# The weights' sums of the last product are queued behind taps and spread over the up projection; the held products and the outputs at the end get a fixed order

## The chip, the cores and the metric

The kernel runs on one NeuronCore of a Trainium2 chip. The metric is the device time of one execution in microseconds, as the median of several runs. The engines are TensorE (PE in the profile, with its weight loads as PEld), VectorE (DVE), ScalarE (ACT) and GpSimd (POOL); SyncE (SP) only issues DMAs here. Each engine takes its instructions in the order of its own queue, and a DMA is issued by an instruction that stands in the queue of SP, ACT or POOL.

## The reference, cut to what matters

The kernel computes one layer of a streaming encoder for 512 tokens of width 1024: four parallel mixers with gates, a cross-attention into 256 memory tokens, and a gated MLP. Only the MLP is touched by the change:

```
hf = rms_norm(x, norm_ffn_pre)                            # 512 x 1024
u = dwconv_causal(hf @ w_up, ffn_dw) + ffn_dw_b           # w_up 1024 x 5632, taps of width 3 per channel
u_g, u_v = split(u, 2, axis=-1)                           # 2816 each
yff = (silu(u_g) * u_v) @ w_down                          # w_down 2816 x 1024
x = x + rms_norm(yff, norm_ffn_post)
```

All of it is float32.

## The kernel before

Every product is made of three matmuls in a rounded format (`mm3`): each operand is split into a high part (a cast, on ACT) and a low part (a subtraction, mostly on DVE), and high x high, high x low and low x high are added up in PSUM. Weights are loaded as float32 by SP into raw tiles `wr` (2 buffers), and cast (L183) and subtracted (L184) into `wh` and `wl` (4 buffers each), three jobs ahead of the product that uses them (`run_blocks`).

The kernel is written in program order, but a planner, which simulates the engines, lays out the order of each engine's instructions: what is ready early in its simulation may be put ahead of what is written before it. On the chip the queues then keep that order, and semaphores make them wait.

**Up projection** (`up_jobs`). The 5632 channels come as 44 chunks of 128, n = 0 to 43, taken alternately from the gate half (i = 0) and the value half (i = 1). One chunk is one group of 24 matmuls of 128 x 512 (8 blocks of the width 1024, three matmuls each). The products go to four PSUM banks, two of tag `mm` and two of tag `av`, in turn, so that a group needs the bank of the group four before it. In `done`, ACT writes the bank into `c` with the last tap and the bias (L1290), and DVE adds the two other taps from the bank (`taps`, L519); after that the bank is free. Behind a value chunk come tanh (L1294), two products on DVE (L1295, L1297) into the tiles `qa` or `qb`, and behind every second of these POOL makes sums of activations (`activation_sums`, L1338 to L1341).

**Down projection** (`down_jobs`). The product with `w_down` is made by a scheme with seven products of half size in place of eight (Strassen's, in Winograd's form). The 22 blocks of 128 rows of `w_down` are taken as 11 pairs. For each pair four sums of the weights' quarters are needed. They are made ahead, during the up projection: `weight_pair(q)` has POOL load two blocks into two tiles `wp` (tag `dw`, 4 buffers), `weight_sums(q)` has DVE make four sums in place (L1351 to L1354) and POOL store the tiles to a DRAM tensor `sums` (L1356). In program order `weight_sums(q)` follows `done` of chunk n = 6 + 3q, and `weight_pair(q + 1)` follows that. The tag `dw` is later used by the down projection's own raw tiles, which SP loads (L1373) from `w_down` and from `sums`, and which ACT (L1378) and DVE (L1379) split into `wh` and `wl`, or, for one of the sums, into a tile `n4` in the space of a used-up `qa`.

The down projection has two phases over the 11 pairs. Phase 0 has four products per pair (M1, M6, M5, M7), two tiles of 128 rows each; phase 1 has three (M2, M3, M4). Activations are split into slots in the space of `hth` and `htl`, 4 of them. In phase 1 the products of the last four pairs are held back (`hold`) and made at the end, one result after the other, in `ends`: `whole` makes the 12 held matmuls of one result in one bank and adds the bank to what phase 0 left (L1491); `result` has ACT square it with a sum per row (L1428), POOL make the norm's factor (L262, L265) where both halves of a token tile are there, and DVE multiply by the gain (L1467); `finish` has DVE multiply by the factor and add the residual (L1476), and SP store it (L1477). There are four token tiles of 128; M4 belongs to tiles 2 and 3, M2 and M3 to tiles 0 and 1.

Of the kernel before, what the change touches and what calls it, by code (L numbers as in the profile page):

```python
# [16 lines left out]
F32 = mybir.dt.float32  # L17
F32R = mybir.dt.float32r
AF = mybir.ActivationFunctionType
ALU = mybir.AluOpType  # L20
# [4 lines left out]
P = 128  # L25
S = 512
D = 1024
# [6 lines left out]
NF = DFF // P  # L34
# [48 lines left out]
def hybrid_layer(ctx: ExitStack, tc: tile.TileContext, a: dict, out: bass.AP):  # L83
    nc = tc.nc
    V, A, G, PE, SP = nc.vector, nc.scalar, nc.gpsimd, nc.tensor, nc.sync
# [22 lines left out]
    w_up, w_down = a["w_up"][0], a["w_down"][0]  # L108
# [19 lines left out]
    for i in range(8):  # L128
        n = ("wh", "wl")[i % 2]
# [3 lines left out]
        elif i < 6:  # L133
            n = ("fz_raw", "fz", "fe", "fu", "fd")[i - 1]
# [7 lines left out]
    def weights_tile(kind):  # L142

        i = w_used[kind]
        w_used[kind] += 1
        return w_tiles.pop((kind, i), None) or gp.tile([P, WB], F32R, tag=f"{kind}{i % 4}", name=kind)
# [43 lines left out]
    def cols(w, c0, n=P, k0=0, nk=NK):  # L190

        return w[k0 * P:(k0 + nk) * P, c0:c0 + n].rearrange("(k p) c -> p k c", p=P), [P, nk, n]
# [104 lines left out]
    m1 = tc.tile_pool(name="m1", bufs=1)  # L297
# [181 lines left out]
    def pc(name, j=0, n=1):  # L479
        i, base = where[name]  # L480
        return par[i][:, base + j:base + j + n]
# [33 lines left out]
    def taps(dst, src, w, n):  # L515

        for k in range(n - 1):
            s = n - 1 - k
            V.scalar_tensor_tensor(dst[:, s:], src[:, :S - s], w(k), dst[:, s:], ALU.mult, ALU.add)  # L519


    conv_u, conv_y = y8(F32), y8(F32)
# [744 lines left out]


    sums = dram.tile([NF // 2 * P, 2 * D], F32, name="sums")

    def open_ffn():
        bg.drain("n1")
# [10 lines left out]
    def up_jobs():  # L1283
        st, held = {}, []

        def done(j, i, ps):
            if i == 0:
                st[j] = ns.fp.tile([P, 2, S], F32, tag="c", name="c", bufs=2)
            c, ch = st[j], i * NF + j
            A.activation(c[:, i], ps, AF.Identity, bias=pc("fb", ch), scale=pc("fdw2", ch))  # L1290
            taps(c[:, i], ps, lambda k: pc("fdw01", k * 44 + ch), 3)
            if i == 1:
                th = ns.fp.tile([P, S], F32, tag="th", name="th")
                A.activation(th, c[:, 0], AF.Tanh, scale=0.5)  # L1294
                V.scalar_tensor_tensor(th, th, 1.0, c[:, 0], ALU.add, ALU.mult)  # L1295
                x = ns.quart[j // 2]
                V.scalar_tensor_tensor(x[j % 2][:, 0:2].rearrange("p a b -> p (a b)"), th, 0.5, c[:, 1],  # L1297
                                       ALU.mult, ALU.mult)
                if j % 2:
                    activation_sums(*x)  # L1300


        for n in range(2 * NF):
            def body(hi, lo, n=n):
                j, i = divmod(n, 2)
                if n > 3:
                    ps = bank()
                    channel_major(ps, (hi, lo), ns.hf)
                    done(j, i, ps)
                    if n % 3 == 0 and n // 3 - 2 < NF // 2:  # L1310
                        weight_sums(n // 3 - 2)
                        if n // 3 - 1 < NF // 2:
                            weight_pair(n // 3 - 1)
                    return
                if n == 0:
                    bg.drain("n0")
                ps = bank(("mm", "sc")[n % 2])
                (channel_major if n else by_pass)(ps, (hi, lo), ns.hf, slice(0, S // 2))
                held.append((j, i, ps, (hi, lo)))
                if n == 3:  # L1320
                    open_ffn()
                    for j, i, ps, w in held:
                        (channel_major if i or j else by_pass)(ps, w, ns.hf, slice(S // 2, S))
                        done(j, i, ps)
                    weight_pair(0)
            yield *cols(w_up, n % 2 * DFF + n // 2 * P), body, V, same, HALF_SHIFT if n < 4 else 0


# [12 lines left out]
        G.tensor_tensor(z[:, 2], z[:, 0], x[:, 1], ALU.subtract)  # L1341

    def weight_pair(q):
        ns.pair = [ns.fp.tile([P, D], F32, tag="dw", name="wp", bufs=4) for _ in range(2)]
        for i in range(2):
            G.dma_start(ns.pair[i], w_down[(2 * q + i) * P:(2 * q + i + 1) * P, :])

    def weight_sums(q):

        (b11, b12), (b21, b22) = ((x[:, :S], x[:, S:]) for x in ns.pair)  # L1350
        V.tensor_tensor(b22, b22, b12, ALU.subtract)  # L1351
        V.tensor_tensor(b12, b12, b11, ALU.subtract)
        V.tensor_tensor(b11, b22, b11, ALU.add)
        V.tensor_tensor(b21, b21, b11, ALU.subtract)  # L1354
        for i in range(2):
            G.dma_start(sums[q * P:(q + 1) * P, i * D:(i + 1) * D], ns.pair[i])  # L1356

    def down_jobs():
        pairs, hold, half = NF // 2, 4, S
# [21 lines left out]
        def activations(phase, q):  # L1381

            if (phase, q) == (0, 0):
                hi, lo = (gp.tile([P, WB], F32R, tag="wr", name="wr", bufs=2) for _ in range(2))
            else:
                if "slots" not in parts:
                    parts["slots"] = [t[:, i * 4:i * 4 + 4].rearrange("p a b -> p (a b)") for t in new_ht()
                                      for i in range(2)]
                slot = parts["slots"][(phase * pairs + q - 1) % 4]
                hi, lo = slot[:, :D], slot[:, D:]  # L1390
            n = 4 - phase
            hi, lo = hi[:, :n * 256], lo[:, :n * 256]
            split_to(hi, lo, ns.quart[q][phase].rearrange("p a b -> p (a b)"))
            form = dict(a=n, b=256)
            parts[phase, q] = hi.rearrange("p (a b) -> p a b", **form), lo.rearrange("p (a b) -> p a b", **form)

        def weights(phase, q, job):
            n = 2 * (phase * pairs + q) + job
            load(n + 3)
            if job == 0:  # L1400
                activations(phase, q)
            raw = raws[n]
            if (phase, job) == (1, 1):
                both = ns.fp.tile([P, D], F32R, tag=f"qa{q}", name="n4")
                both = both[:, :half], both[:, half:]
                split_to(*both, raw[:, :half])
                return [both],
            hi, lo = weights_tile("wh")[:, :D], weights_tile("wl")[:, :D]
            split_to(hi, lo, raw)
            return [(hi[:, i * half:(i + 1) * half], lo[:, i * half:(i + 1) * half]) for i in range(2)],  # L1410

# [46 lines left out]
        def result(t, i, x, dst, pieces=1):  # L1458

            ms[t, i] = square(x, i, pieces)  # L1460
            r = None
            if (t, 1 - i) in ms:
                *early, last = ms[t, 1 - i] + ms[t, i]
                if len(early) == 2:
                    G.tensor_tensor(early[0], early[0], early[1], ALU.add)
                r = rstd_of(ns.fp, [early[0], last])
            V.tensor_tensor(dst, x, ns.post[:, gains[i]], ALU.mult)  # L1467
            return r

        def finish(t, halves, r):  # L1470
            for i in halves:
                o = halves[i]
                n = S // 2 if (t, i) == (1, 1) else S
                for c in range(0, S, n):
                    d = slice(i * S + c, i * S + c + n)
                    V.scalar_tensor_tensor(o[:, c:c + n], o[:, c:c + n], r, ns.out[t][:, d], ALU.mult, ALU.add)  # L1476
                    SP.dma_start(out[t * P:(t + 1) * P, d], o[:, c:c + n])  # L1477

        def ends():

            m1, u, z7, z = (parts[n] for n in ("m1", "u", "z7", "z"))

            def whole(name, t, x, pieces=1):

                for c in range(pieces):
                    cut = slice(c * S // pieces, (c + 1) * S // pieces)
                    for q, job, ws in held:
                        for (n, a), w in zip(work[1, job], ws):
                            if n == name:
                                step(name, t, q, a, w, 1, cut)  # L1490
                    V.tensor_tensor(x[:, cut], x[:, cut], banks[name][t][:, cut], ALU.add)  # L1491
                return x

            for t in range(2):
                x = whole("M4", t, z7[:, t])
                finish(2 + t, {1: z[:, t], 0: x}, result(2 + t, 0, x, x))
            for t in range(2):
                x = whole("M2", t, m1[:, t])
                result(t, 0, x, x)
                x = whole("M3", t, u[:, t])  # L1500
                finish(t, {0: m1[:, t], 1: x}, result(t, 1, x, x))

        def body(phase, q, job, ws):
            if (phase, q, job) == (0, 0, 0):
# [66 lines left out]
```

## Time and profile before

| | |
|---|---|
| median of 3 runs | 1074.48 us (1073.96 to 1076.75) |
| profiled execution, its own time | 1080.23 us |
| its span | 1078.4 us |
| granted TensorE clock, mean | 0.995 |
| up projection, first full group to last | 735.8 to 962.3 us |
| 24 matmuls of 128 x 512 in a row | 5.44 us |
| last output issued | 1073.1 us |

The profile is of one execution. Times are in microseconds from the start of the span. A line of a timeline gives start, duration, engine, line of the kernel, operation, what it writes and reads, and in brackets the idle time of the engine ahead of it with what ended that. Instructions on one engine overlap a little, so the distance between two starts is shorter than a duration: 0.227 us between two matmuls whose records last 0.39, and 0.60 us between two DVE additions of 128 x 512 whose records last 0.69. PE's ends are modelled. Some matmul records are missing.

### The profile page before, as it was taken

The page shows a single profiled execution, that of the slowest core. Times are in us where ns is not written, and L with a number is a line of the kernel's source. Part 1 is how long each engine was busy: PE and PEld are TensorE (multiplying, and loading weights), DVE is VectorE, ACT ScalarE, POOL GpSimd, SP SyncE. Part 2 cuts the span into 40 slices and gives each one's busy share as a digit, 9 for nine tenths or more (in the row PEclk, how much of TensorE's full clock was granted, in tenths as well). Part 3 has the DMA queues.
Part 4 walks back from the last instruction along what each step waited for, and adds up shares of the span by engine and source line. Part 5 has one row for each costly group of instructions (what it writes and reads, how often), then busy time and mean ns, then how long its engine had stood idle before and what let it go on. Part 6 is the DMA issues. An engine that isn't in the chain of part 4 may idle for free.

```text
span 1078.4 us, 14440 instructions
## 1 busy us (share of the span) xinstructions
PE 1058.9 (98%) x5387; PEld 899.4 (83%) x5387; DVE 758.1 (70%) x1211; ACT 488.5 (45%) x809; POOL 172.7 (16%) x277
## 2 busy tenths in 40 slices
PE   9999999999999999999999999999998999999995
PEld 8888888888888988888888899998886788888884
DVE  7899996466666467767464486868778686677785
ACT  5322222467464365655443265644322343445671
POOL 4000001000101023323000130132333121111002
PEclk9999999999999999999999999999999999999998
DMA  6433433332222243233255343146889843226662
GB/s 203 117 98 91 90 105 95 94 98 78 59 81 79 63 134 98 79 98 115 62 176 173 120 139 97 59 154 215 268 285 292 269 118 98 79 78 192 215 189 78
DMA packets 158523, 141.04 MB, mean 131 GB/s; under 512 B 5055, under 2 KB 134700, under 8 KB 158453
## 3 DMA queue, kind: packets, MB, share of 16 engines
q1 hardware_dynamic: 149555, 108.50, 34.2%
q0 software_dynamic: 8896, 31.61, 8.8%
q8 instruction: 42, 0.69, 0.3%
q14 instruction: 28, 0.23, 0.1%
q10 hardware_dynamic: 2, 0.00, 0.0%
HBM read 126.45 MB, written 13.65 MB: 130 GB/s over the span
## 4 chain that ended last, share of the span: by engine, by line
PE 85%; DMA 7%; DVE 3%; issue 2%; POOL 1%; ACT 1%; POOLq 0%; DVEq 0%; ACTq 0%
PE ps_mm L225 45%; PE ps_av L225 25%; PE ps_sc L225 7%; DMA sums<-wp 4%; PE ps_tr L229 3%; PE ps_tr L225 2%; DMA wp<-in_w_down 2%; DVE wl L184 1%; PE ps_mm L432 1%; ACT wh L183 0%; DVE c L519 0%; PE ps_av L432 0%; PE ps_mm L374 0%; DMA wr<-in_w_gate 0%; DMA wr<-in_w_in 0%
## 5 line engine op out<-in xcount | busy, mean ns | idle before, releaser
L183 ACT CAST wh<-wr 128x1024 fp32r<-128x1024 f32 (+1 forms) x150 | 156.9, 1048 | 289.0 <-PE ps_mm L225 140.3
L184 DVE TENSOR_TENSOR wl<-wr,wh 128x1024 fp32r<-128x1024 f32 (+1 forms) x150 | 186.0, 1242 | 112.8 <-ACT wh L183 112.4
L225 PE MATMUL ps_mm<-hth,wh 128*128 128x512 f32 (+1 forms) x616 | 231.6, 382 | 4.3 <-DVE c L519 3.8
L225 PE MATMUL ps_mm<-hth,wl 128*128 128x512 f32 (+1 forms) x616 | 230.0, 380 | 0.0
L225 PE MATMUL ps_mm<-htl,wh 128*128 128x512 f32 (+1 forms) x616 | 229.9, 380 | 0.0
L225 PEld LDWEIGHTS ps_mm<-hth,wh 128*128 128x128 f32 x616 | 114.3, 188 | 25.9 <-issue 4.6
L225 PEld LDWEIGHTS ps_mm<-hth,wl 128*128 128x128 f32 x616 | 114.0, 188 | 21.1
L225 PEld LDWEIGHTS ps_mm<-htl,wh 128*128 128x128 f32 x616 | 114.1, 188 | 20.4 <-DVE htl L153 0.2
L225 PE MATMUL ps_av<-hth,wh 128*128 128x512 f32 (+1 forms) x328 | 123.3, 376 | 2.5 <-DVE c L519 2.5
L225 PE MATMUL ps_av<-htl,wh 128*128 128x512 f32 (+1 forms) x328 | 123.0, 375 | 0.0
L225 PE MATMUL ps_av<-hth,wl 128*128 128x512 f32 (+1 forms) x328 | 122.8, 374 | 0.0
L585 DVE SCALAR_TENSOR_TENSOR y<-y,par,y 128x499 f32<-128x499 f32 (+28 forms) x120 | 82.4, 730 | 0.2
L225 PEld LDWEIGHTS ps_av<-hth,wh 128*128 128x128 f32 x328 | 62.0, 189 | 13.9 <-ACT c L1290 2.9
L225 PEld LDWEIGHTS ps_av<-hth,wl 128*128 128x128 f32 x328 | 62.0, 189 | 11.1
L225 PEld LDWEIGHTS ps_av<-htl,wh 128*128 128x128 f32 x328 | 62.1, 189 | 10.8
L225 PE MATMUL ps_mm<-y,wh 128*128 128x512 f32 x192 | 61.2, 394 | 0.0
L1379 DVE TENSOR_TENSOR wl<-dw,wh 128x1024 fp32r<-128x1024 f32 x33 | 41.4, 1260 | 13.4 <-ACT wh L1378 13.3
L1378 ACT CAST wh<-dw 128x1024 fp32r<-128x1024 f32 x33 | 34.5, 1052 | 23.2 <-PE ps_tr L225 8.4
L1294 ACT ACTIVATE th<-c 128x512 f32<-128x512 f32 x22 | 13.9, 632 | 62.4 <-DVE c L519 59.7
L225 PEld LDWEIGHTS ps_mm<-y,wh 128*128 128x128 f32 x192 | 35.4, 188 | 6.8
L908 POOL TENSOR_SCALAR fbias<-ck,cq 128x128 f32<-128x128 f32 (+3 forms) x32 | 27.4, 861 | 68.3 <-DVE st L914 60.5
L225 PE MATMUL ps_mm<-y,wl 128*128 128x512 f32 x96 | 37.6, 392 | 0.0
(426 smaller groups left out, 2026.3 us busy)
## 6 DMA issues: line engine op xcount, KB each, us to landing
wr<-in_w_up SPq DMA_DIRECT2D x44, 512.0 KB
wr<-in_w_in SPq DMA_DIRECT2D x38, 512.0 KB
wr<-in_w_gate SPq DMA_DIRECT2D x32, 512.0 KB
wp<-in_w_down POOLq DMA_DIRECT2D x22, 512.0 KB, 6.2
sums<-wp POOLq DMA_DIRECT2D x22, 512.0 KB, 7.2
dw<-sums SPq DMA_DIRECT2D x44, 256.0 KB
wr<-in_w_branch SPq DMA_DIRECT2D x16, 512.0 KB
dw<-in_w_down SPq DMA_DIRECT2D x11, 512.0 KB
```

The source lines that it names most:

```text
L183: order(A.copy(hi, raw[:, :n]))
L184: low.tensor_tensor(lo, raw[:, :n], hi.bitcast(F32), ALU.subtract)
L225: PE.matmul(ps, lhs, rhs, start=start, stop=stop)
L229: PE.transpose(ps, x, ident[:n, :n])
L432: keep(PE.matmul(banks[c][:, :S // 2], w[p == 1][:, k, c * P:(c + 1) * P], ht[p == 2][:, i * 4 + k, :S // 2], start=(i, p, k) == (0, 0, 0) ...
L585: V.scalar_tensor_tensor(dst[:, s:], src[:, :S - s], pc("conv_dw", k * 4 + j), dst[:, s:], ALU.mult, ALU.add)
L908: G.tensor_scalar(bias[:, :w], ck[j][:, :w], -1.0, cq[:, qt, head:head + 1], ALU.mult, ALU.add)
L1294: A.activation(th, c[:, 0], AF.Tanh, scale=0.5)
L1378: A.copy(hi, x)
L1379: V.tensor_tensor(lo, x, hi.bitcast(F32), ALU.subtract)
```

## The change

`taps` now gives back its last instruction, and `done` keeps it. The DVE instructions of `weight_sums(q)` are bound to stand behind the last tap instruction of chunk n = 6 + 3q on DVE's queue (`tc.issue_after`), so that the planner cannot lay them ahead of it. `weight_pair` is called two pairs ahead in place of one: pairs 0 and 1 both after chunk 3, and pair q + 2 after the sums of pair q.

In the down projection the last pair's activations of phase 1 go to tiles in the space of `qa0` and `qa1`, and its split weights to two tiles of the tag `dw`, where before they took the next slot and the next `wh` and `wl`.

In `ends` the order is written out and kept on PE, DVE, ACT and POOL (`tc.manual_schedule`): M4 of tile 2, M4 of tile 3, then M2 and M3 of tile 0, M2 and M3 of tile 1. The outputs of a token tile (`finish`) stand behind the addition, square and gain of the next product.

```
--- before.py
+++ after.py
@@ -516,7 +516,8 @@
 
         for k in range(n - 1):
             s = n - 1 - k
-            V.scalar_tensor_tensor(dst[:, s:], src[:, :S - s], w(k), dst[:, s:], ALU.mult, ALU.add)
+            ins = V.scalar_tensor_tensor(dst[:, s:], src[:, :S - s], w(k), dst[:, s:], ALU.mult, ALU.add)
+        return ins
 
 
     conv_u, conv_y = y8(F32), y8(F32)
@@ -1267,6 +1268,7 @@
 
 
     sums = dram.tile([NF // 2 * P, 2 * D], F32, name="sums")
+    ns.pair = {}
 
     def open_ffn():
         bg.drain("n1")
@@ -1288,7 +1290,7 @@
                 st[j] = ns.fp.tile([P, 2, S], F32, tag="c", name="c", bufs=2)
             c, ch = st[j], i * NF + j
             A.activation(c[:, i], ps, AF.Identity, bias=pc("fb", ch), scale=pc("fdw2", ch))
-            taps(c[:, i], ps, lambda k: pc("fdw01", k * 44 + ch), 3)
+            st["last"] = taps(c[:, i], ps, lambda k: pc("fdw01", k * 44 + ch), 3).ins
             if i == 1:
                 th = ns.fp.tile([P, S], F32, tag="th", name="th")
                 A.activation(th, c[:, 0], AF.Tanh, scale=0.5)
@@ -1307,10 +1309,12 @@
                     ps = bank()
                     channel_major(ps, (hi, lo), ns.hf)
                     done(j, i, ps)
-                    if n % 3 == 0 and n // 3 - 2 < NF // 2:
-                        weight_sums(n // 3 - 2)
-                        if n // 3 - 1 < NF // 2:
-                            weight_pair(n // 3 - 1)
+                    q = n // 3 - 2
+                    if n % 3 == 0 and q < NF // 2:
+                        with tc.issue_after(st["last"]):
+                            weight_sums(q)
+                        if q + 2 < NF // 2:
+                            weight_pair(q + 2)
                     return
                 if n == 0:
                     bg.drain("n0")
@@ -1323,6 +1327,7 @@
                         (channel_major if i or j else by_pass)(ps, w, ns.hf, slice(S // 2, S))
                         done(j, i, ps)
                     weight_pair(0)
+                    weight_pair(1)
             yield *cols(w_up, n % 2 * DFF + n // 2 * P), body, V, same, HALF_SHIFT if n < 4 else 0
 
 
@@ -1341,19 +1346,20 @@
         G.tensor_tensor(z[:, 2], z[:, 0], x[:, 1], ALU.subtract)
 
     def weight_pair(q):
-        ns.pair = [ns.fp.tile([P, D], F32, tag="dw", name="wp", bufs=4) for _ in range(2)]
+        pair = ns.pair[q] = [ns.fp.tile([P, D], F32, tag="dw", name="wp", bufs=4) for _ in range(2)]
         for i in range(2):
-            G.dma_start(ns.pair[i], w_down[(2 * q + i) * P:(2 * q + i + 1) * P, :])
+            G.dma_start(pair[i], w_down[(2 * q + i) * P:(2 * q + i + 1) * P, :])
 
     def weight_sums(q):
 
-        (b11, b12), (b21, b22) = ((x[:, :S], x[:, S:]) for x in ns.pair)
+        pair = ns.pair.pop(q)
+        (b11, b12), (b21, b22) = ((x[:, :S], x[:, S:]) for x in pair)
         V.tensor_tensor(b22, b22, b12, ALU.subtract)
         V.tensor_tensor(b12, b12, b11, ALU.subtract)
         V.tensor_tensor(b11, b22, b11, ALU.add)
         V.tensor_tensor(b21, b21, b11, ALU.subtract)
         for i in range(2):
-            G.dma_start(sums[q * P:(q + 1) * P, i * D:(i + 1) * D], ns.pair[i])
+            G.dma_start(sums[q * P:(q + 1) * P, i * D:(i + 1) * D], pair[i])
 
     def down_jobs():
         pairs, hold, half = NF // 2, 4, S
@@ -1382,6 +1388,8 @@
 
             if (phase, q) == (0, 0):
                 hi, lo = (gp.tile([P, WB], F32R, tag="wr", name="wr", bufs=2) for _ in range(2))
+            elif (phase, q) == (1, pairs - 1):
+                hi, lo = (ns.fp.tile([P, D], F32R, tag=f"qa{i}", name="a3") for i in range(2))
             else:
                 if "slots" not in parts:
                     parts["slots"] = [t[:, i * 4:i * 4 + 4].rearrange("p a b -> p (a b)") for t in new_ht()
@@ -1405,7 +1413,10 @@
                 both = both[:, :half], both[:, half:]
                 split_to(*both, raw[:, :half])
                 return [both],
-            hi, lo = weights_tile("wh")[:, :D], weights_tile("wl")[:, :D]
+            if (phase, q) == (1, pairs - 1):
+                hi, lo = (ns.fp.tile([P, D], F32R, tag="dw", name="dwr", bufs=4) for _ in range(2))
+            else:
+                hi, lo = weights_tile("wh")[:, :D], weights_tile("wl")[:, :D]
             split_to(hi, lo, raw)
             return [(hi[:, i * half:(i + 1) * half], lo[:, i * half:(i + 1) * half]) for i in range(2)],
 
@@ -1491,14 +1502,19 @@
                     V.tensor_tensor(x[:, cut], x[:, cut], banks[name][t][:, cut], ALU.add)
                 return x
 
-            for t in range(2):
-                x = whole("M4", t, z7[:, t])
-                finish(2 + t, {1: z[:, t], 0: x}, result(2 + t, 0, x, x))
-            for t in range(2):
-                x = whole("M2", t, m1[:, t])
-                result(t, 0, x, x)
-                x = whole("M3", t, u[:, t])
-                finish(t, {0: m1[:, t], 1: x}, result(t, 1, x, x))
+            waiting = None
+            with tc.manual_schedule(engines={e.engine for e in (PE, V, A, G)}):
+                for name, t, i, x in (("M4", 0, 0, z7), ("M4", 1, 0, z7), ("M2", 0, 0, m1), ("M3", 0, 1, u),
+                                      ("M2", 1, 0, m1), ("M3", 1, 1, u)):
+                    token = t + 2 * (name == "M4")
+                    x = whole(name, t, x[:, t])
+                    r = result(token, i, x, x)
+                    if waiting:
+                        finish(*waiting)
+                        waiting = None
+                    if r is not None:
+                        waiting = token, {1: z[:, t], 0: x} if name == "M4" else {0: m1[:, t], 1: x}, r
+                finish(*waiting)
 
         def body(phase, q, job, ws):
             if (phase, q, job) == (0, 0, 0):
```

## The prediction

> **What bounds the kernel now.** I read the page first: its head and the busy time of TensorE (PE).
>
> ```profile
> span 1078.4 us, 14440 instructions
> PE 1058.9 (98%) x5387; PEld 899.4 (83%) x5387; DVE 758.1 (70%) x1211; ACT 488.5 (45%) x809; POOL 172.7 (16%) x277
> ```
>
> PE is busy for 98% of the span: only a place where PE waits, or what lies behind its last matmul, can give time back. So next came the waits, PE's own for the whole run, then all engines' for 725 to 860 us (engine, line, waited for: us in total, times, longest).
>
> ```profile
> PE ps_mm L225 <- DVE c L519: 3.8, 2, 2.3
> PE ps_av L225 <- DVE c L519: 2.5, 1, 2.5
> ...
> ACT wh L183 <- DMA wr<-in_w_up: 38.4, 12, 7.0
> POOL wp L1346 <- DMA sums<-wp: 35.8, 13, 6.6
> DVE wp L1351 <- DMA wp<-in_w_down: 14.1, 5, 4.8
> ```
>
> PE waits three times for taps (L519), which free its banks, and all three lie in the up projection. VectorE (DVE) itself waits for down weights (L1351), GpSimd (POOL) for stores of sums, ScalarE (ACT) for up weights. The timelines of DVE, then PE, around the longest one (start, duration, in brackets idle before and releaser):
>
> ```profile
> 834.06 1.52 DVE L519 SCALAR_TENSOR_TENSOR c<-ps_mm,par,c 128x510 f32<-128x510 f32 x2
> 840.37 0.69 DVE L1351 TENSOR_TENSOR wp<-wp 128x512 f32<-128x512 f32 x1 [4.79 <-DMA wp<-in_w_down]
> ...
> 845.30 0.75 DVE L519 SCALAR_TENSOR_TENSOR c<-ps_av,par,c 128x511 f32<-128x511 f32 x1
> ```
>
> ```profile
> 843.30 0.39 PE L225 MATMUL ps_mm<-hth,wl 128*128 128x512 f32 x1
> 846.19 0.76 PE L225 MATMUL ps_av<-hth,wh 128*128 128x512 f32 x1 [2.51 <-DVE c L519]
> 846.75 0.63 PE L225 MATMUL ps_av<-htl,wh 128*128 128x512 f32 x1
> ```
>
> The sums stand ahead of taps on DVE's queue. DVE sits 4.79 us until the weights land, the taps end at 846.05, and PE starts at 846.19. The windows of 20 us show why the weights land late (PE, PEld, DVE, ACT, POOL busy; clock; DMA share; GB/s):
>
> ```profile
> 820.00:840.00 20.00, 17.68 (x79) 14.32 (x78) 14.20 (x19) 6.32 (x8) 7.07 (x12) 1.00 0.91 286
> 840.00:860.00 20.00, 17.49 (x71) 14.09 (x70) 14.81 (x20) 5.82 (x7) 4.91 (x6) 0.91 0.88 280
> 900.00:920.00 20.00, 20.00 (x90) 16.54 (x89) 11.84 (x15) 7.86 (x10) 2.94 (x4) 1.00 0.36 105
> ```
>
> The planner runs all 11 pairs between 732 and 846, one per 10.4 us, and the DMA engines are 0.9 busy; afterwards they idle. Last, the end:
>
> ```profile
> 1066.82 0.39 PE L225 MATMUL ps_tr<-wh,hth 128*128 128x512 f32 x1
> ...
> 1068.15 0.74 DVE L1476 SCALAR_TENSOR_TENSOR o<-o,st_r,res 128x512 f32<-128x512 f32 x1
> 1068.81 0.68 DVE L1491 TENSOR_TENSOR o<-o,ps_tr 128x512 f32<-128x512 f32 x1
> ```
>
> The last addition starts 1.76 us after PE is done (1067.05, 0.23 after the last matmul's start), because outputs of the token tile before it stand ahead on DVE.
>
> **The change, part by part.**
>
> *Sums behind taps (moved).* Each pair issues 4 DVE subtractions or additions (0.60 us apart, 2.4 us), two stores from POOL (0.54 us each, 7.2 us to landing) and later two loads (0.54 each, 6.2 to landing). Pair q now runs behind the taps of group n = 6+3q, one pair per three groups of 24 matmuls (3 x 5.44 = 16.3 us), the last at n = 36. The work is the same; it moves past taps on DVE and stands ahead only of later ones.
> What it removes: the three PE waits. Start to start, PE loses 1.88-0.23, 2.72-0.23 and 2.89-0.23 us, that is 1.65+2.49+2.66 = 6.80. Behind the first two, one start each is 0.08 late: 0.15. Behind the third, eight starts take 3.50 us in place of 8 x 0.227 = 1.81 (granted clock 0.50 from 847 to 849): 1.69. Sum 8.64 us.
> [...]
>
> *What is late next.* DVE's load per three groups: three splits at 1.14, six taps at 0.66, three products of a chunk (two per two groups, 0.60 each, 1.8), sums 2.4: 11.6 of 16.3 us, so taps keep up. DMA: up weights 0.52 MB per 5.44 us are 96 GB/s, a pair's 2.10 MB per 16.3 us are 129, together 225 against 280 to 307 in the stretch that stalls.
>
> *Loads two pairs ahead (moved).* Pair q+2 takes pair q's buffers: store 7.2 and load 6.2 end 13.4 us after sums q, and sums q+2 come 32.6 us after them. Its wait stands on POOL, ahead of the activation sums (L1338 to 1341), which nobody needs before the down projection. Pairs 0 and 1 are loaded at 721 to 724 as now. Cost nothing, cover 19 us.
>
> *Later first loads of the down projection.* They reuse pairs 9 and 10's buffers, so SP's queue issues them not at 842 but when those are stored: group 4 starts at 735.8, so group 36 ends at 735.8+33 x 5.44 = 915.3, taps 2.3, sums 2.4, store 7.2: 927; landed by 934. The first split of down weights, now at 946.9, comes at about 938. Cost nothing, by 4 us and the weights that are cast three groups ahead.
>
> *Buffers for the last pair, order of the end.* Pair 10's split weights and activations go to tiles that are free, so ACT no longer waits for PE (0.24 us at 1049.57, off the path). In the fixed order, PE's 72 held matmuls take 72 x 0.2267 = 16.32 us, as now; the first product needs pair 10 after nine of them, 2.0 us in. Those activations are ready 2.0 us in now, with that wait ahead of them: no loss. DVE does per product an addition, a wait for ACT's square, a multiplication (1.53+0.61 = 2.14 us); a finish adds 1.32. From the second product's end at 5.44: 3.46+3.46+2.14+3.46 = 12.52, so the last addition starts 17.96 us in, 1.64 after PE's end against 1.76 now. Gain 0.12 us; bounds are 1.76 (DVE free at PE's end) and -1.7 (one finish and one wait for ACT more ahead of it).
>
> Sum: 1080.23 - 8.64 - 0.12 = 1071.5 for the profiled execution. That one lies 5.75 us above the median of the runs shown (1074.48). PE has no other gap over 0.3 us than these waits, the first 1.3 us and the tail, so a part of the 5.75 may be longer waits, as they hang on DMA landings. Bounds: none of it (gain 8.76, 1065.7) or all (3.0, 1071.5). The nearest row is the spread of the runs, 1076.75-1074.48 = 2.27: I take the waits as that much shorter in a median run. 1074.48 - 8.76 + 2.27 = 1068.0.
>
> **The rivals.**
>
> *A part of the waits stays.* For it: ACT waits 38.4 us for up weights, not touched directly. Against: from 860 on, with the DMA engines under half busy, PE does not wait once. Half of 6.4 (8.64 less 2.27) stays: 1068.0+3.2 = 1071.2.
>
> *No effect.* DVE's order changes but DMA, not order, holds the taps; or a new wait takes the sum. Against it: L1351 itself shows the wait. 1074.5.
>
> *Slower: up weights behind down loads on SP.* SP's queue is in order, and the planner may place the loads that wait for pair 10's store ahead of the last up weights; it placed down loads among them at 842 to 854. Then after group 36: taps 2.3, sums 2.4, store 7.2, landing 6.2, cast and split 2.3 = 20.4 us until the next weights, less 5.44 for each group whose weights were issued already. Now the last of 44 up loads is issued at 932.2, when PE is in group 38 of 43, so 4.6 are ahead and nothing shows. With one ahead PE loses 15.0 and the time is 1068.0+15.0 = 1083.0; it decides from two ahead down (9.5 lost, 1077.5).
>
> *More.* DVE is free at PE's end and the waits are as in the profile: 1074.48-8.64-1.76 = 1064.1.
>
> **How the numbers follow.** A measurement can tell about 0.3%, 3.2 us: 1071.3 to 1077.7 is no change. Forecast 0.62 (own range 1065.7 to 1071.5), a part stays 0.12, no effect 0.08, slower by SP's queue 0.10, more 0.08. The range 1063.5 to 1074.5 leaves out the slower case and edges. Faster: 0.62+0.08 and 0.08 of the part case, 0.78; same 0.12; slower 0.10.
>
> **What the profile after would show.** Right: no wait of PE on L519, no wait of L1351 on DMA, the last sums after 915, clock 1.00 throughout, DMA share near 0.7 from 760 to 920, the last addition 1.6 us behind PE. Wrong: PE waiting for weights between groups 37 and 43, for taps elsewhere, or at the start of the held products.

## The result, and the profile after

The changed kernel takes 1071.42 us as the median of 20 runs (1070.42 to 1075.30), the kernel before 1077.59 in 20 runs beside them (1073.96 to 1084.59). The ratio is 0.9942, 95% interval 0.9928 to 0.9957: 6.2 us faster, and the whole interval lies beyond the 0.3% that the prediction counts as no change. The profiled execution took 1070.76 us, its span 1069.0, against 1080.23 and 1078.4 before.

The page of the changed kernel: span, busy time, and the chain that ended last by engine, which gave PE 85% and DMA 7% before.

```profile
span 1069.0 us, 14449 instructions
PE 1056.0 (99%) x5387; PEld 898.2 (84%) x5387; DVE 764.4 (72%) x1211; ACT 489.2 (46%) x809; POOL 171.1 (16%) x277
...
PE 98%; DVE 1%; ACT 0%; issue 0%; POOL 0%; POOLq 0%; DVEq 0%; ACTq 0%
```

The waits of the changed kernel, PE's own for the whole run, then two lines of all engines' for 720 to 960 us (waited for: us in total, times, longest). Lines have moved by a few: the sums are now L1357 to L1360.

```profile
PE ps_mm L374 <- DVE e L325: 1.3, 1, 1.3
PE ps_mm L225 <- ACT hth L152: 0.2, 1, 0.2
...
POOL wp L1351 <- DMA sums<-wp: 28.4, 15, 3.3
ACT wh L183 <- DMA wr<-in_w_up: 1.4, 2, 1.0
```

PE waits for the first operands and 0.2 us once; no wait for taps is left. DVE has no wait for down weights in this stretch, and ACT's for up weights has gone from 38.4 us (725 to 860) to 1.4. DVE's timeline at one pair (start, duration), and the windows of 20 us that answer to those before (PE, PEld, DVE, ACT, POOL busy; clock; DMA share; GB/s):

```profile
835.07 1.53 DVE L519 SCALAR_TENSOR_TENSOR c<-ps_av,par,c 128x510 f32<-128x510 f32 x2
836.51 0.69 DVE L1357 TENSOR_TENSOR wp<-wp 128x512 f32<-128x512 f32 x1
...
840.61 0.68 DVE L1360 TENSOR_TENSOR wp<-wp 128x512 f32<-128x512 f32 x1
841.21 1.52 DVE L519 SCALAR_TENSOR_TENSOR c<-ps_mm,par,c 128x510 f32<-128x510 f32 x2
```

```profile
820.00:840.00 20.00, 20.00 (x90) 16.57 (x89) 16.54 (x22) 8.17 (x10) 6.51 (x9) 1.00 0.66 211
840.00:860.00 20.00, 20.00 (x90) 16.57 (x89) 16.02 (x21) 6.46 (x9) 5.36 (x9) 1.00 0.72 224
900.00:920.00 20.00, 20.00 (x90) 16.57 (x89) 16.33 (x22) 6.56 (x9) 4.45 (x6) 1.00 0.67 215
```

The first line counts two tap instructions; the first sum of the pair starts right behind the second, with no idle time ahead of it. PE is busy through every window, and the DMA work that stood in 745 to 855 is spread to 920. The end of the two engines' timelines:

```profile
1056.79 0.84 PE L225 MATMUL ps_tr<-dwr,a 128*128 128x512 f32 x3
...
1058.67 0.74 DVE L1487 SCALAR_TENSOR_TENSOR o<-o,st_r,res 128x512 f32<-128x512 f32 x1
1059.34 0.68 DVE L1502 TENSOR_TENSOR o<-o,ps_tr 128x512 f32<-128x512 f32 x1
```

PE is done at 1057.47 (three matmuls of 0.227 from 1056.79) and the last addition starts 1.87 us later, behind two outputs of the tile before, much as before (1.76).

The two spans differ by 9.4 us. 8.64 are the three waits and what stood behind them; 0.86 had been lost before already ahead of the up projection (its second halves begin at 724.78 before and at 723.92 after), in code that the change leaves as it is; 0.11 go the other way at the end. 8.64+0.86-0.11 = 9.39.

### The profile page after: what moved, and what is told of

The parts are those of the page before. It is cut to its first block, busy times and chain, and to the rows that moved or that the text cites. A ratio compares the mean times of both kernels' runs of the same rounds, so it can differ in the third digit from the quotient of the medians.

```text
span 1069.0 us, 14449 instructions
## 1 busy us (share of the span) xinstructions
PE 1056.0 (99%) x5387; PEld 898.2 (84%) x5387; DVE 764.4 (72%) x1211; ACT 489.2 (46%) x809; POOL 171.1 (16%) x277
## 4 chain that ended last, share of the span: by engine, by line
PE 98%; DVE 1%; ACT 0%; issue 0%; POOL 0%; POOLq 0%; DVEq 0%; ACTq 0%
PE ps_mm L225 52%; PE ps_av L225 30%; PE ps_sc L225 8%; PE ps_tr L229 3%; PE ps_tr L225 2%; PE ps_mm L432 1%; PE ps_av L432 1%; PE ps_mm L374 0%; ACT junk L1439 0%; DVE o L1487 0%; PE ps_sc L379 0%; DVE wr L1487 0%; DVE wr L1478 0%; DVE z L1487 0%; DVE o L1502 0%; DVE wr L1502 0%
## 5 line engine op out<-in xcount | busy, mean ns | idle before, releaser
L184 DVE TENSOR_TENSOR wl<-wr,wh 128x1024 fp32r<-128x1024 f32 (+1 forms) x150 | 189.2, 1263 | 113.1 <-ACT wh L183 112.7
L1385 DVE TENSOR_TENSOR wl<-dw,wh 128x1024 fp32r<-128x1024 f32 x32 | 40.2, 1261 | 12.3 <-ACT wh L1384 12.2
```

Of the source, the lines that this page charges most:

```text
L184: low.tensor_tensor(lo, raw[:, :n], hi.bitcast(F32), ALU.subtract)
L1385: V.tensor_tensor(lo, x, hi.bitcast(F32), ALU.subtract)
```

## The experiments

Each kernel was run beside the kernel before; a ratio is to that.

**Only the up projection's part.** `ends` and the last pair's buffers as before; the rest as changed.

> Only the up projection's part of the change: sums behind the taps of chunk 6+3q, loads two pairs ahead; the buffers and the order of the end are as before. Theory (the gain is PE's waits in the up projection): no wait of PE on taps, time as the changed kernel's within 2 us (about 1071.5), ratio to before 0.993 to 0.996; the last addition starts 1.7 us after PE's end, as in both. Rival (the fixed end carries a good part of the gain): ratio nearer to 1, 0.997 or more.

Median 1071.33 (10 runs) against 1079.35, ratio 0.9933 (0.9910 to 0.9957): the whole gain. The profiled execution (1074.96 us) has none of the waits on taps, but a wait of another kind, which comes back below:

```profile
PE ps_sc L225 <- DVE st L915: 1.9, 1, 1.9
```

**Only the end's part.** The up projection as before.

> Only the end's part of the change: the last pair's own buffers and the fixed order of the held products and outputs; the up projection is as before. Theory: PE's waits on taps are there as before (4 to 9 us in all with the slow matmuls behind them), the tail differs by 0.1 us, ratio 0.998 to 1.002. Rival (the end carries the gain): ratio 0.997 or less.

Median 1078.75, ratio 0.9994 (0.9967 to 1.0021): nothing measurable. The waits on taps are there; its PE timeline at the longest:

```profile
826.12 0.39 PE L225 MATMUL ps_av<-hth,wl 128*128 128x512 f32 x1
828.58 0.77 PE L225 MATMUL ps_mm<-hth,wh 128*128 128x512 f32 x1 [2.07 <-DVE c L519]
829.14 0.63 PE L225 MATMUL ps_mm<-htl,wh 128*128 128x512 f32 x1
```

Start to start, PE loses 2.23 us here, 1.63 to eight slow matmuls behind it (granted clock 0.62 from 828 to 830 and 0.53 from 830 to 832), and 0.46 at a second wait: 4.3 us in all.

**Order without the earlier loads, and earlier loads without order.** Both have the end as before. The first keeps `issue_after` and loads one pair ahead, the second loads two pairs ahead and leaves the sums to the planner.

```
-                        if q + 2 < NF // 2:
-                            weight_pair(q + 2)
+                        if q + 1 < NF // 2:
+                            weight_pair(q + 1)
...
-                    weight_pair(1)
```

> Sums behind the taps, but loads one pair ahead as before; end as before. Theory (the place of the sums on VectorE's queue is the cause, and the loads' ring of four buffers is the same either way): PE's waits on taps are gone, ratio as with the up projection's whole part, 0.993 to 0.996. Rival (the loads two pairs ahead are needed): VectorE waits for down weights again, some us per pair, but now behind taps; PE waits again in part, ratio 0.997 to 1.0.

```
-                        with tc.issue_after(st["last"]):
-                            weight_sums(q)
+                        weight_sums(q)
```

> Loads two pairs ahead, but nothing binds the sums to stand behind the taps; end as before. The planner lays out sums and taps on VectorE in the same sequence as in the kernel before. Theory (order is the cause): PE's waits on taps remain, 4 to 9 us, ratio 0.998 to 1.002. Rival (early loads take the wait away): VectorE no longer waits for down weights, ratio 0.993 to 0.996.

Order alone: 1073.87 (9 runs), ratio 0.9939 (0.9912 to 0.9965), no wait of PE on taps and none of DVE on down weights. Earlier loads alone: 1078.84, ratio 0.9988 (0.9964 to 1.0012), and its waits (the first sum is L1356 here) are like those of the kernel before:

```profile
ACT wh L183 <- DMA wr<-in_w_up: 47.3, 12, 9.2
...
DVE wp L1356 <- DMA wp<-in_w_down: 14.1, 5, 3.3
...
PE ps_mm L225 <- DVE c L519: 5.0, 2, 2.5
```

DVE's sequence of taps and sums in this kernel is that of the kernel before, instruction by instruction. So the binding carries the gain, and the call two pairs ahead does nothing measurable. But the binding sets two things at once: sums come behind taps, and, since pair q waits for chunk 6 + 3q, a pair comes only every 16.3 us. The next two kernels take these apart.

**Order near the old pace.** The changed kernel with two chunks per pair in place of three.

```
-                    q = n // 3 - 2
-                    if n % 3 == 0 and q < NF // 2:
+                    q = n // 2 - 3
+                    if n % 2 == 0 and 0 <= q < NF // 2:
```

> The changed kernel with pair q's sums behind the taps of chunk 6+2q in place of 6+3q: one pair per two groups, 10.9 us, about the pace of the kernel before (10.4), but with VectorE's order kept. Theory (order: sums must not wait ahead of older taps): PE waits on taps for under 1 us, ratio to before 0.993 to 0.996 as with the changed kernel, though the DMA engines are 0.85 to 0.95 busy again. Rival (the pace, that is the load on the DMA engines, made the waits): ScalarE waits 20 us or more for up weights again, PE waits 4 us or more on taps, ratio 0.998 or more.

1074.14 in 5 runs, which lie at 1071 and at 1074 to 1075.5; ratio 0.9933 (0.9909 to 0.9957). A window of its profile and a line of its waits:

```profile
820.00:840.00 20.00, 20.00 (x90) 16.57 (x89) 17.76 (x23) 8.18 (x10) 7.52 (x11) 1.00 0.92 287
```

```profile
ACT wh L183 <- DMA wr<-in_w_up: 1.3, 2, 0.8
```

The DMA engines are 0.92 busy, as in the kernel before (0.91), and yet PE never waits for taps, and ACT waits 1.3 us for up weights. So a DMA share of 0.92 does not by itself make the waits. ACT's 38 us of waits before also went at that load; they fit as a consequence of DVE's waits, since DVE's splits free the raw tiles that the up weights are loaded into, but that was not tried by itself.

The pace is not quite the old one, though. From first sum to first sum it is 10.0 to 11.5 us here. In the kernel before, the 10.4 us of the prediction are a mean that takes in a pause of 26.8 us ahead of pair 2 (pairs count from 0); from pair 2 to pair 10 the steps are 6.0 to 12.2 us, 9.8 on average (762.30 to 840.37). The first sums of its pairs 8 and 9, with pair 10's following at 840.37:

```profile
821.32 0.82 DVE L1351 TENSOR_TENSOR wp<-wp 128x512 f32<-128x512 f32 x1 [2.74 <-DMA wp<-in_w_down]
828.60 0.68 DVE L1351 TENSOR_TENSOR wp<-wp 128x512 f32<-128x512 f32 x1
```

**One pair per chunk.** `q = n - 6`, for every n from 6 on.

> The same with one pair per group, chunk 6+q, 5.4 us: faster than the ring of four buffers can turn (sums 2.4, store 7.2, load 6.2 for two pairs: 8 to 10 us per pair). Theory (what harms is VectorE standing at the sums for a late load with taps behind it): VectorE waits at the first sum of nearly each pair, 25 us or more in all, PE loses 10 to 35 us, although each pair stands behind the taps of its own chunk. If order alone were the whole matter, PE would lose nothing.

One execution, 1075.52 us. Its waits:

```profile
ACT wh L183 <- DMA wr<-in_w_up: 28.8, 14, 5.5
...
DVE wp L1357 <- DMA wp<-in_w_down: 12.5, 6, 4.3
...
PE ps_mm L225 <- DVE c L519: 2.5, 2, 1.4
...
PE ps_av L225 <- DVE c L519: 1.3, 1, 1.3
```

The sign was right and the size was not: DVE waits again and PE loses 4.5 us (start to start), not 10 to 35. The sums of the 11 pairs start from 754.7 to 853.8, 9.9 us apart on average: the planner, free to put them later than the bound, spread them to about the pace of the kernel before, which the expectation had overlooked. What follows is a sharper form of the theory. Standing behind the taps of one's own chunk is not the point in itself, since here each pair does and PE waits all the same. The point is that DVE comes to a sum only when its load has landed.

A pair is loaded into the buffers of the pair two before it, so what counts is how much stands on DVE's queue between the sums of the two. With two chunks per pair it is eight tap instructions each time, four groups or 21.8 us of PE, and DVE never waits; in the changed kernel it is twelve or thirteen. With one pair per chunk it is four to eight: at the six pairs with six or fewer DVE waits every time (at one of them the profile names no cause), at the three with seven or eight once. In the kernel before it is five to eight from pair 2 on, most often six; there the pairs with seven and eight wait too, and one with six does not. Six are three groups, 16.3 us of PE, and 2.4 us of sums, 7.2 to the store's landing and 6.2 to the load's (both medians of the kernel before) are 15.8: next to nothing to spare. One pair per chunk ran only once, and no run gives the pairs more room without binding them, so that room is the cause is in part argued.

**A better end.** The outputs of the tile before are put where DVE waits for ACT's square, between the addition and the multiplication of the next product.

```
+            if between:
+                finish(*between)
             V.tensor_tensor(dst, x, ns.post[:, gains[i]], ALU.mult)
...
-                    r = result(token, i, x, x)
-                    if waiting:
-                        finish(*waiting)
-                        waiting = None
+                    r = result(token, i, x, x, between=waiting)
+                    waiting = None
```

> The changed kernel with one thing moved at the end: a token tile's two output instructions stand between the addition and the multiplication of the next product, where VectorE waits for ScalarE's square, and not behind the multiplication. Theory (VectorE's chain of 3.46 us per product is the bound behind PE's end): a product costs VectorE 0.61+1.32+0.61 = 2.54 us, under PE's 2.72, the last addition starts within 0.3 us of PE's end in place of 1.7, 1.5 us less than the changed kernel, ratio to before 0.9925. Rival (the chain is bound elsewhere, by GpSimd's factor or the stores): 0.3 us or less.

1069.66 (6 runs), ratio 0.9912 (0.9892 to 0.9931). Its end, DVE and PE:

```profile
1057.15 0.75 DVE L1489 SCALAR_TENSOR_TENSOR o<-o,st_r,res 128x512 f32<-128x512 f32 x1
1057.81 0.69 DVE L1480 TENSOR_TENSOR wr<-wr,g_ffn 128x512 f32<-128x512 f32 x1
1058.60 0.69 DVE L1504 TENSOR_TENSOR o<-o,ps_tr 128x512 f32<-128x512 f32 x1
```

```profile
1057.72 0.84 PE L225 MATMUL ps_tr<-dwr,a 128*128 128x512 f32 x3
```

PE is done at 1058.40 and the last addition starts 0.20 later, in place of 1.87. A second set of 6 runs:

> The filled gap alone again. Both theories: two levels, near 1069.6 and 1074, the upper one in about a third of the runs.

1069.48, ratio 0.9914 (0.9886 to 0.9943). Of these 12 runs ten lie between 1069.2 and 1071.0, with a median of 1069.5, and two at 1074. The changed kernel's own lower runs, under 1073.2, have a median of 1071.2, so the gain over it is about 1.7 us, near the 1.5 expected; the two kernels were not run beside each other. Over both sets this is the fastest kernel of the study.

**The two levels.** Most runs of the kernels with the binding fall near 1071 (1069.5 with the better end) or near 1075 (1074); a few lie between. Near 395 us, in the mixer, attention waits for a row that POOL stores to DRAM (`crows`) and loads again (`ck`). Waits for 380 to 410 us, first of the changed kernel (1070.76 us), then of the up projection's part alone (1074.96):

```profile
POOL ck L879 <- DMA crows<-e: 1.6, 1, 1.6
```

```profile
POOL ck L879 <- DMA crows<-e: 3.6, 1, 3.6
...
PE ps_sc L225 <- DVE st L915: 1.9, 1, 1.9
```

Where the store takes 2 us more to land, PE waits, and slow matmuls follow (granted clock 0.58 and 0.57 from 398 to 402). Seven of the profiled executions of kernels with the binding took 1074.7 to 1075.6 us: this wait is there in all but the one with one pair per chunk, which has the waits on taps in its place. In the four under 1071 us it is not. The binding is not what brings it: the end's part alone, with the old order, has it in its profile too (PE on L915 1.6 us, behind 3.8 us for `crows`). So the kernel with the better end was also given a later due time for that attention step.

```
-        yield 0.0, 2.0
+        yield 0.0, 5.0
```

> The same as the one with the filled gap, and the planner's due time for the first step of the forgetting attention is 5.0 in place of 2.0, so that the products come later behind the load of ck from DRAM. Theory (the two levels of the changed kernel's times, 1071 and 1075, are the wait of PE on VectorE's L915 near 395 us, 1.9 us with 2 us of slow matmuls behind it, when that load lands late): no such wait, all runs at 1069 to 1070. Rival (the levels have another cause): two levels remain; or the new order makes waits elsewhere.

All 5 runs low, 1069.27 to 1070.44; but two thirds of the runs with the old due time are low too, so it was run again.

> The kernel with the filled gap and the later due time again, beside the one with the filled gap alone. Theory (the upper level of the times is PE's wait for the load of ck near 395 us): no run on the upper level. Rival (5 of 5 low runs were chance, since about two thirds of all runs with the old due time are low too): a third of the runs near 1074.

1071.80, six runs from 1069.77 to 1074.67, and the profile of the highest shows the same wait (PE on L915, 2.0 us, behind 3.5 us for `crows`). The later due time does not take it away; the five low runs were most likely chance. That a late landing of `crows` goes with the upper level is shown by the profiles; what makes the store land late was not found.

**The fixed order without the last pair's buffers,** and the changed kernel beside it.

> The changed kernel without the own buffers of the last pair: its activations and split weights of phase 1 take the next slot and the next wh and wl, as before, while the fixed order of the end stays. Theory (cost and gain of the buffers are near nothing, since the first held product needs the last pair 2.0 us after it begins): ScalarE waits for PE under 1 us again, PE waits at most 1.5 us at the first held product, time within 1.5 us of the changed kernel. Rival (without them the fixed order starves PE): PE waits 3 us or more there.

> The changed kernel itself, on the same chip as the one without the buffers. Theory: 1071 or 1075 in single runs, two levels 4 us apart; the ratio to before 0.992 to 0.996, no wait of PE on taps.

1072.34 and 1072.90, ratios 0.9946 (0.9924 to 0.9969) and 0.9950 (0.9929 to 0.9971): the same. Without the buffers ACT waits 0.17 us for PE again, and neither profile has a wait of PE behind 730 us. The buffers are worth nothing measurable here.

## Why the prediction was right, point by point

**The three waits** were the gain, and all three went, with the slow matmuls behind them. Only the binding of the sums brings it, as the parts alone show.

**The size.** The prediction took 8.76 us off the profiled execution and gave 2.27 back, since a median run's waits should be shorter: 6.5 us, a ratio of 0.9940. Measured is 0.9942. That the waits vary was right: in other executions with DVE's old sequence PE loses 6.7 us (earlier loads alone) and 4.3 (the end's part alone) in place of 8.64. The 2.27 itself is the spread of three runs and measures no wait; that it came so near is partly luck, the more so as part of the spread has another source, the next point.

**The time itself** came out 3.4 us later than the 1068.0 forecast, at the upper edge of the likeliest case's own range. The step that failed is the base, "1074.48 - 8.76 + 2.27": the three runs of before that were shown lie at the low end. Twenty runs give 1077.59, 3.1 us more, and the other sets of before 1077.7 to 1080.7. The prediction saw the run-to-run difference only as lengths of the up projection's waits; the second source, the late `crows`, lies in code that the change doesn't touch and shows in no profile of before that was at hand.

**What is late next.** DVE, DMA and POOL kept up as worked out. The DMA share is 0.66 to 0.75 from 760 to 920 (0.7 forecast, GB/s 211 to 248 against 225), the last sums start at 918 to 922 (after 915), and the first split of down weights is at 937.3 (938).

**The slower rival** did not come. SP's queue in the changed kernel:

```profile
912.45 0.38 SPq L169 DMA_DIRECT2D wr<-in_w_up  x1
912.88 0.75 SPq L1379 DMA_DIRECT2D dw<-sums  x1
917.06 5.55 SPq L169 DMA_DIRECT2D wr<-in_w_up  x2
925.15 0.34 SPq L1379 DMA_DIRECT2D dw<-in_w_down  x1
```

Down loads do stand between up loads, but those for pair 10's buffers are issued at 925.2 (927 forecast), behind the last up weights at 922.6. At that time PE is in group 38 of 43, as in the kernel before. Neither of the two cases in which waits stay or the change does nothing came about. The time alone could not tell: 1071.42 is nearly the 1071.2 that the prediction gave for a part of the waits staying. What decides is the profile, which has no wait on taps, and the runs beside the kernel before.

**The end.** The chain of DVE's steps was forecast at 12.52 us from the second product's addition to the last; it took 12.55 (1046.79 to 1059.34). The gain of 0.12 was not there, since the addition at which the chain begins starts 0.2 us behind its matmuls (1046.79 against 1046.58), which the sum had left out. The runs agree that the end's part is worth nothing measurable.

**Where the reason was too simple.** The text put the harm in the order of taps and sums, and named the busy DMA engines as the reason for late loads. Two chunks per pair, at 0.92 DMA share, show that the share does no harm by itself; one pair per chunk shows that the order does not help by itself either. Taken together, the sums have to be placed with time to spare behind their load, and the prediction's mean of one pair per 10.4 us hid how little the kernel before left of it. The prediction got the gain right because three groups per pair leave room enough, not because its reason for the late loads was complete.

## What to carry to other kernels

On DVE here, an instruction that waited for a DMA held up the taps that stood behind it (4.79 us at 840.37 in the kernel before); where PE needs the results behind it, bind the waiting instruction to a point that PE itself paces, and leave more time between two turns of the buffers than the turn takes on the chip (15.8 us here by the sum above), not in the planner. Try the parts of a change alone: here one part of four carried the gain, and the fixed order at the end paid only once the outputs were moved into the gaps where VectorE waits for ScalarE (0.79 to 0.85 us each in the changed kernel): about 1.7 us. Where single waits of a few microseconds come and go, the median of three runs lay 3.1 us below that of twenty (1074.48 against 1077.59).

## What was unexpected of the hardware

In these profiles the length of a wait did not decide whether PE's granted clock fell to half behind it. In the kernel before, 1.50 and 2.33 us idle were followed by full speed (clock 1.00, 0.23 us from start to start) and 2.51 by half (0.50 from 847 to 849, 0.43 us from start to start); with the end's part alone 2.07 us were followed by half (0.53 from 830 to 832); with earlier loads alone 2.51 us were followed by full speed (1.00 from 828 to 832):

```profile
828.43 0.47 PE L225 MATMUL ps_mm<-hth,wh 128*128 128x512 f32 x1 [2.51 <-DVE c L519]
828.73 0.40 PE L225 MATMUL ps_mm<-htl,wh 128*128 128x512 f32 x1
```

A limit between 2.33 and 2.51 us, as the one execution of the kernel before could suggest, therefore does not hold in the others. Near 395 us all seven waits on L915, 1.6 to 2.6 us long, were followed by matmuls 0.43 us apart, six of them with a second wait of 0.3 us close behind. The slow stretch did not always begin where the wait ended, either: in the second profile of the changed kernel PE goes on at 397.55, matmuls start 0.31 and 0.23 us apart from 398.36 on, and only from 399.27 on 0.43 apart. The slow stretch behind a wait for taps was nearly as long both times: 3.50 us in the kernel before (846.19 to 849.69) and 3.44 (828.58 to 832.02) with the end's part alone. What sets off the half clock was not found. An estimate from these two, 1.69 us lost behind 2.51 and 1.63 behind 2.07: a wait of 2 to 2.5 us on PE counts 1.6 to 1.7 us more here, but not every time.
